# In the second gate/up chunk, the rests of the last ordinary weight pair no longer queue behind the last pair of seven products

## The chip, the core and the metric

The kernel runs on one core of a Trainium2 chip. The metric is the device time of one execution in microseconds (us), as the median of the executions shown. The engines are named as in the profile: PE is TensorE (PEld its weight loads), DVE is VectorE, ACT is ScalarE, POOL is GpSimd and SP is SyncE, which issues most of the transfers.

## What is computed

Two layers of an encoder trunk, for 256 tokens of width 2048 in float32. The part that matters here is the SwiGLU block, with `w_gate` and `w_up` of 2048 x 5632:

```
def swiglu(h, w_gate, w_up, w_down):
    return (jax.nn.silu(h @ w_gate) * (h @ w_up)) @ w_down

def reference(x, w_in, w_o, ..., w_gate, w_up, w_down):
    for l in range(DEPTH):
        h = rms_norm(x, pre_mix_norm[l])
        m = hybrid_mixer(h, l, w_in[l], w_o[l], ...)
        x = x + rms_norm(m, post_mix_norm[l])
        h = rms_norm(x, pre_ffn_norm[l])
        f = swiglu(h, w_gate[l], w_up[l], w_down[l])
        x = x + rms_norm(f, post_ffn_norm[l])
    return x
```

## The kernel before

**Weights.** All weights are laid out in one stream of 128 x 1024 float32 pieces (512 KB), in the order in which they are used. A piece holds 256 rows (`kp`, eight of them) of 512 columns (`c`, the chunk; eleven for gate and up). The stream's index is part of a tile's name. In layer 0, 144 to 159 are the gate and up pieces of chunk 1 in turn, and 160 to 175 those of chunk 2. Layer 1 has the same pattern 392 places further on.

**Rounding.** Each float32 product is made of three products of a rounded part and a rest. For an ordinary piece, `feed` lets ScalarE round it (`hi<-raw`, L310) and VectorE take the difference, the *rest* (`lo<-raw,hi`, L320). `raw` has four buffers, `hi` and `lo` six each. The next piece can be fetched into a `raw` buffer once the rest of the piece in it is made.

**Ordinary pairs and sevens.** An ordinary gate/up pair takes eight blocks of products on TensorE (`eight`, L1255). For some `kp` (in chunk 1: 5 and 6, in chunk 2: 2, 4, 5 and 6) seven products stand for the eight (`seven_products`, L1137 to L1139), as in Strassen's scheme. For these, the up piece `T` arrives in two transfers: a plain one that SP issues (L258), and an accumulation of half the gate piece on top, issued on POOL's queue (L259), which waits for the first. The gate piece is `G` (L231). `mixed_weights` then makes the sums of the two, each with a rounded part and a rest:

- `hi<-T` (ACT L280) and `lo<-T` (DVE L282)
- `T<-T` (DVE L291) and `G<-G,T` (DVE L292), the sums
- `Th<-T` (ACT) and `Tl<-T` (DVE), half a piece, then `Th<-G` and `Tl<-G`, a whole one. The last of the seven products read these.

**Who decides the order.** A scheduler places the instructions of every engine, by its own estimates. `tc.issue_after` keeps an instruction behind another one in this order, without a wait on a semaphore. `held` is a pair of such an instruction and a count: `behind` puts the next ordinary rests, as many as the count, behind it. In chunk 1 the pairs are used in turn, 0 to 7. Pairs 5 and 6 are sevens, pair 7 (pieces 158 and 159) is the last and ordinary one. When the weights of pair 6 have been prepared, `mixed_weights` sets `held` to that piece's last rest, `Tl<-G`, for two rests, which are lo158 and lo159. The set `last_of_row` names the pieces after which this is done: the up piece of pair 6 of chunk 1, one in each layer.

**Other work near by.** For two gate pieces of each chunk, the second and third, POOL makes the rest (`helped`, L313). After the chunk's last seven, `shared_part` (L1178 to L1182) combines the sums that the products share. At the chunk's end VectorE adds these to the accumulators (L1433, L1437), ScalarE applies silu (L1434), and VectorE multiplies (L1439). The result of the chunk before is transposed on TensorE (L1372) near the chunk's end, and ScalarE copies it out of the accumulator bank (L1373).

**Transfers.** `fetch` gives out the transfers in the stream's order, and the scheduler places them on SP. `not_ahead` keeps a transfer of the sevens (`G` and `T`) behind an ordinary one at least six pieces earlier. `put_away` (L396) sends a quarter of the residual to memory once in each of four chunks.

Of the kernel before, what the change touches and what calls it, by code (L numbers as in the profile page):

```python
# [45 lines left out]
NEXT_SEVEN = (5, 6)  # L46
# [34 lines left out]
def weight_order():  # L81

    order = []

    def queue_pair(name, l, kp, c):
        order.append((name, l, kp, c))
        return len(order) - 1

    plan = []
    sevens, plain, own = set(), set(), set()  # L90
    for l in range(L):
        lay = {"in": {}, "o": {}, "gate": {}, "up": {}, "down": {}}
        for n, (ca, cb) in enumerate(PAIRS):
            for kp in IN_ORDER if n else range(KT // 2):
                lay["in"][ca, kp] = queue_pair("w_in", l, kp, ca)
                lay["in"][cb, kp] = queue_pair("w_in", l, kp, cb)
                if kp in IN_NOW[n]:
                    plain.add(lay["in"][cb, kp])
        order_o = [(c, kp) for kp in KP_O for c in (0, 1)]
        order_o += [(c, kp) for kp in LATE_O for c in (2, 3)] + [(c, kp) for c in (2, 3) for kp in LAST_O]  # L100
        lay["order_o"] = order_o
        for c, kp in order_o:
            lay["o"][c, kp] = queue_pair("w_o", l, kp, c)
            if c == 3 and kp in O_SEVEN:
                own.add(lay["o"][c, kp])
        for c in range(FF // CW):
            for kp in gate_order(c):
                lay["gate"][c, kp] = queue_pair("w_gate", l, kp, c)
                lay["up"][c, kp] = queue_pair("w_up", l, kp, c)
                if kp in gate_sevens(c):  # L110
                    sevens.add(lay["up"][c, kp])
        for half in range(2):
            for kp in range(FF // P // 2):
                for c in (2 * half, 2 * half + 1):
                    lay["down"][c, kp] = queue_pair("w_down", l, kp, c)
                if kp in DOWN_SEVEN[half]:
                    sevens.add(lay["down"][2 * half + 1, kp])
        plan.append(lay)
    return order, plan, sevens, plain, own
# [48 lines left out]
def kernel(  # L168
# [35 lines left out]
    order, plan, sevens, plain, own = weight_order()  # L204
# [5 lines left out]
            for n in (1, 2):  # L210
                helped[lay["gate"][c, gate_order(c)[n]]] = n == 1
    newest_seven = [None]
    last_of_row = {lay["up"][1, NEXT_SEVEN[-1]] for lay in plan}

    ready = {}
    raws, loads = [], []
# [47 lines left out]
    def mixed_weights(i):  # L264

        g, u = raws[i - 1], raws[i]
        hi = wpool.tile([P, 2, CW], F32R, tag="hi", bufs=6, name=f"hi{i}")
        lo = wpool.tile([P, 2, CW], F32R, tag="lo", bufs=6, name=f"lo{i}")
        if i in own:
            th = wpool.tile([P, 2, CW], F32R, tag="hi", bufs=6, name=f"Th{i}")  # L270
            tl = wpool.tile([P, 2, CW], F32R, tag="lo", bufs=6, name=f"Tl{i}")
            th2 = mix_pool[0].tile([P, 2 * (S + P)], F32R, tag="ah", bufs=1, name=f"T2h{i}")[:, 0:CW]
            tl2 = mix_pool[0].tile([P, 2 * (S + P)], F32R, tag="al", bufs=1, name=f"T2l{i}")[:, 0:CW]
        else:
            th = mix_pool[0].tile([P, 3, CW], F32R, tag="Th", bufs=1 if i in plain else 2, name=f"Th{i}")
            tl = mix_pool[0].tile([P, 3, CW], F32R, tag="Tl", bufs=1 if i in plain else 2, name=f"Tl{i}")
            th2, tl2 = th[:, 2, :], tl[:, 2, :]

        def split(h, l, w):
            nc.scalar.activation(h, w, AF.Copy)  # L280
            with in_row(i):
                newest_rest[i] = nc.vector.tensor_tensor(out=l, in0=w, in1=h.bitcast(F32), op=ALU.subtract)  # L282

        if i in plain or i in own:
            with after_rests():
                nc.vector.tensor_tensor(out=u[:, 0, :], in0=g[:, 0, :], in1=u[:, 0, :], op=ALU.add)
        split(hi, lo, u)
        t1, b22 = ((hi[:, k, :], lo[:, k, :]) for k in range(2))
        t3, t4 = ((th[:, k, :], tl[:, k, :]) for k in range(2))
        t2 = u[:, 1, :]  # L290
        nc.vector.tensor_tensor(out=t2, in0=t2, in1=u[:, 0, :], op=ALU.subtract)  # L291
        nc.vector.tensor_tensor(out=g, in0=g, in1=t2.unsqueeze(1).to_broadcast([P, 2, CW]), op=ALU.add)  # L292
        split(th2, tl2, t2)
        split(th[:, 0:2, :], tl[:, 0:2, :], g)
        if i in last_of_row:
            held[:] = newest_rest[i], 2
        t2 = th2, tl2
        return {"b22": b22, "t1": t1, "t2": t2, "t3": t3, "t4": t4}

    def feed(upto):  # L300
        fetch(upto)
        while fed[0] < min(upto, len(stream)):
            i = fed[0]
            raw = raws[i]
            if i in sevens or i in plain or i in own:
                ready[i] = mixed_weights(i)
                fed[0] += 1
                continue
            hi = wpool.tile([P, 2, CW], F32R, tag="hi", bufs=6, name=f"hi{i}")
            nc.scalar.activation(hi, raw, AF.Copy)  # L310
            lo = wpool.tile([P, 2, CW], F32R, tag="lo", bufs=6, name=f"lo{i}")
            if i in helped:
                rest = nc.gpsimd.tensor_tensor(out=lo, in0=raw, in1=hi.bitcast(F32), op=ALU.subtract)  # L313
                if helped[i]:
                    tc.add_manual_dep(rest.ins, newest_seven[0].ins.name, AFTER, reason="the shared port")
                ready[i] = (hi, lo)
                fed[0] += 1
                continue
            with behind():
                rest = nc.vector.tensor_tensor(out=lo, in0=raw, in1=hi.bitcast(F32), op=ALU.subtract)  # L320
            ready[i] = (hi, lo)
            fed[0] += 1
            rests.append(rest)
# [21 lines left out]
    held = [None, 0]  # L345
    follows, newest_rest = {}, {}

    def in_row(i):

        return tc.issue_after(follows[i].ins) if i in follows else nullcontext()  # L350
# [8 lines left out]
    def after_rests():  # L359

        return tc.issue_after(rests[-1].ins)
# [826 lines left out]
    for l in range(L):  # L1188
# [27 lines left out]
        for kp in LATE_O[:-1]:  # L1216
            i, j = (plan[l]["o"][c, kp] for c in (2, 3))
# [387 lines left out]
```

## Time and profile before

| What | Value |
|---|---|
| median of 3 runs | 2183.49 us (2182.69 to 2186.39) |
| the profiled execution's own time | 2185.51 us |
| its span, first to last instruction | 2183.8 us |
| granted TensorE clock | 0.999 |
| TensorE busy | 2168.2 us, 99% |
| VectorE busy | 1912.0 us, 88% |
| ScalarE busy | 1392.1 us, 64% |
| GpSimd busy | 256.1 us, 12% |
| read from memory | 460.14 MB, 215 GB/s over the span |

All the details come from the one profiled execution. A row of a timeline has the start in us from the span's beginning, the duration, the engine, the source line, the operation, `out<-in`, the shapes and how many equal instructions are merged (`x4`). In brackets stands how long the engine was idle before it, and what ended that. In the timeline, buffer numbers are left out of the names, so the instructions are told apart by their place.

### The profile page before, as it was taken

Reading aid. Unit: us, or ns where it says so; the run is one execution under the profiler, and the core shown is the slowest. Engines: PE = TensorE matmul, PEld = TensorE weight load, DVE = VectorE, ACT = ScalarE, POOL = GpSimd, SP = SyncE. Lnnn points to the kernel's source line nnn. Section 1 sums busy time; section 2 is a strip of 40 time slices with the busy share of each in tenths; the row PEclk is TensorE's granted clock in tenths of the full one; section 3 lists DMA queues with packets and bytes.
Section 4 is the critical chain, followed back from the end, with each engine's and each line's share of the span. In section 5 each row is a group of like instructions: output and inputs, shape, how many; then the busy total and the mean of one; then the engine's idle time right before and its main releaser. Section 6 shows DMA issues by size and latency. Waiting matters only on the chain.

```text
span 2183.8 us, 28775 instructions
## 1 busy us (share of the span) xinstructions
PE 2168.2 (99%) x9956; PEld 1783.6 (82%) x9956; DVE 1912.0 (88%) x2641; ACT 1392.1 (64%) x2081; POOL 256.1 (12%) x239
## 2 busy tenths in 40 slices
PE   9999999999999999999999999999999999999998
PEld 7888888887888888888878888888888888888886
DVE  7888658889999999999878886588899999999997
ACT  7666665756666666666665666657566666576664
POOL 2100000021222220000010000000222222200000
PEclk9999999999999999999999999999999999999999
DMA  9545555488887777767465555545888877767683
GB/s 336 182 163 174 193 185 177 155 281 247 242 257 229 231 231 236 234 227 254 147 241 174 175 176 186 193 158 179 285 244 237 260 221 230 237 228 242 207 266 100
DMA packets 140274, 470.43 MB, mean 215 GB/s; under 512 B 15952, under 2 KB 16976, under 8 KB 139616
## 3 DMA queue, kind: packets, MB, share of 16 engines
q1 hardware_dynamic: 121952, 436.03, 57.8%
q0 software_dynamic: 17600, 32.02, 8.9%
q8 instruction: 78, 1.28, 0.2%
q10 hardware_dynamic: 576, 0.54, 0.1%
q14 instruction: 68, 0.56, 0.1%
HBM read 460.14 MB, written 8.39 MB: 215 GB/s over the span
## 4 chain that ended last, share of the span: by engine, by line
PE 80%; DVE 11%; issue 3%; DMA 3%; ACT 2%; DVEq 0%; ACTq 0%
PE c L1255 15%; PE in L1137 6%; PE in L1139 6%; PE in L1138 6%; PE dn L1486 4%; PE dn L1487 4%; PE dn L1489 4%; DVE lo L320 3%; PE o L609 2%; PE o L611 2%; PE o L610 2%; DVE Tl L282 2%; PE p L1138 2%; PE c L1138 2%; PE c L1137 2%
## 5 line engine op out<-in xcount | busy, mean ns | idle before, releaser
L320 DVE TENSOR_TENSOR lo<-raw,hi 128x1024 fp32r<-128x1024 f32 x464 | 557.7, 1224 | 105.8 <-ACT hi L310 104.8
L310 ACT ACTIVATE hi<-raw 128x1024 fp32r<-128x1024 f32 x486 | 496.2, 1053 | 86.4 <-DMA raw<-in_weights_in_turn_dram 38.3
L1255 PE MATMUL c<-hi,xF 128*128 128x512 f32 x1344 | 364.0, 392 | 0.9 <-DVE xF L519 0.5
L1255 PEld LDWEIGHTS c<-hi,xF 128*128 128x128 f32 x1344 | 250.2, 188 | 52.6 <-DVE xF L519 1.3
L259 POOL DMA_DIRECT2D T<-in_weights_in_turn_dram x122 | 107.6, 882 | 1394.8 <-PE c L1255 545.2
L1255 PE MATMUL c<-lo,xF 128*128 128x512 f32 x672 | 207.3, 390 | 0.0
L280 ACT ACTIVATE Th<-G 128x1024 fp32r<-128x1024 f32 x122 | 128.8, 1056 | 76.6 <-DVE G L292 75.3
L1486 PE MATMUL dn<-hi,jh 128*128 128x512 f32 x416 | 162.0, 389 | 0.0
L1487 PE MATMUL dn<-lo,jh 128*128 128x512 f32 x416 | 161.8, 389 | 0.0
L280 ACT ACTIVATE Th<-T 128x512 fp32r<-128x512 f32 x122 | 77.2, 633 | 130.2 <-DVE T L291 127.3
L282 DVE TENSOR_TENSOR Tl<-G,Th 128x1024 fp32r<-128x1024 f32 x122 | 149.2, 1223 | 11.3 <-ACT Th L280 11.3
L282 DVE TENSOR_TENSOR lo<-T,hi 128x1024 fp32r<-128x1024 f32 x122 | 155.3, 1273 | 0.7 <-ACT hi L280 0.6
L310 ACT ACTIVATE hi<-G 128x1024 fp32r<-128x1024 f32 x122 | 128.4, 1052 | 36.1 <-DMA G<-in_weights_in_turn_dram 34.5
L292 DVE TENSOR_TENSOR G<-G,T 128x1024 f32<-128x1024 f32 x122 | 148.9, 1221 | 1.8
L1255 PEld LDWEIGHTS c<-lo,xF 128*128 128x128 f32 x672 | 126.0, 188 | 26.3
L320 DVE TENSOR_TENSOR lo<-G,hi 128x1024 fp32r<-128x1024 f32 x104 | 127.0, 1221 | 11.8 <-ACT hi L310 11.7
L280 ACT ACTIVATE hi<-T 128x1024 fp32r<-128x1024 f32 x122 | 128.0, 1049 | 13.3 <-PE c L1139 10.3
L1137 PE MATMUL in<-hi,xT 128*128 128x512 f32 x328 | 131.0, 401 | 0.7 <-ACT hi L942 0.7
L1137 PE MATMUL in<-hi,xI 128*128 128x512 f32 x328 | 131.2, 401 | 0.0
L1138 PE MATMUL in<-lo,xI 128*128 128x512 f32 x328 | 128.0, 390 | 0.3 <-DVE lo L320 0.3
L1489 PE MATMUL dn<-hi,jl 128*128 128x512 f32 x416 | 128.1, 389 | 0.0
L1139 PE MATMUL in<-hi,xI 128*128 128x512 f32 x328 | 128.0, 391 | 0.0
(487 smaller groups left out, 4925.9 us busy)
## 6 DMA issues: line engine op xcount, KB each, us to landing
raw<-in_weights_in_turn_dram SPq DMA_DIRECT2D x498, 512.0 KB, 4.7
T<-in_weights_in_turn_dram SPq DMA_DIRECT2D x122, 512.0 KB, 5.5
G<-in_weights_in_turn_dram SPq DMA_DIRECT2D x122, 512.0 KB, 5.6
T<-in_weights_in_turn_dram POOLq DMA_DIRECT2D x122, 256.0 KB, 5.9
GU<-in_weights_in_turn_dram SPq DMA_DIRECT2D x32, 512.0 KB, 6.5
V<-in_weights_in_turn_dram SPq DMA_DIRECT2D x8, 512.0 KB, 3.8
away_ffn<-x SPq DMA_DIRECT2D x8, 512.0 KB, 8.4
xd<-away_ffn SPq DMA_DIRECT2D x8, 512.0 KB, 8.7
```

What stands on the lines that cost most here:

```text
L280: nc.scalar.activation(h, w, AF.Copy)
L282: newest_rest[i] = nc.vector.tensor_tensor(out=l, in0=w, in1=h.bitcast(F32), op=ALU.subtract)
L292: nc.vector.tensor_tensor(out=g, in0=g, in1=t2.unsqueeze(1).to_broadcast([P, 2, CW]), op=ALU.add)
L310: nc.scalar.activation(hi, raw, AF.Copy)
L320: rest = nc.vector.tensor_tensor(out=lo, in0=raw, in1=hi.bitcast(F32), op=ALU.subtract)
L1137: nc.tensor.matmul(a, sh, hi, start=first, stop=False, skip_group_check=open_sums[0])
L1138: nc.tensor.matmul(a, sh, lo, start=False, stop=False, skip_group_check=open_sums[0])
L1139: return nc.tensor.matmul(a, sl, hi, start=False, stop=last, skip_group_check=open_sums[0])
L1255: nc.tensor.matmul(a, stat[part], w[j][:, kk, :], start=first and kk + n == 0, stop=last and kk == 1 and n == 2)
L1486: nc.tensor.matmul(accs[c, t], sh, hi[:, kk, :], start=first, stop=False, skip_group_check=open_sums[0])
L1487: nc.tensor.matmul(accs[c, t], sh, lo[:, kk, :], start=False, stop=False, skip_group_check=open_sums[0])
L1489: nc.tensor.matmul(accs[c, t], sl, hi[:, kk, :], start=False, stop=last, skip_group_check=open_sums[0])
```

## The change

The two lines that set `held` in `mixed_weights` go, and the set that they ask with them. The rests of pair 7 in chunk 1 then carry no order of their own relative to `Tl<-G` of pair 6, and the scheduler places them by its estimates. The other uses of `held` stay.

```diff
@@ -210,7 +210,6 @@
     newest_seven = [None]
-    last_of_row = {lay["up"][1, NEXT_SEVEN[-1]] for lay in plan}
 
@@ -292,8 +291,6 @@
         split(th2, tl2, t2)
         split(th[:, 0:2, :], tl[:, 0:2, :], g)
-        if i in last_of_row:
-            held[:] = newest_rest[i], 2
         t2 = th2, tl2
```

No instruction is added or removed. The lines behind the edit move up by one to three, so L282 becomes L281, L320 becomes L317, and L242 becomes L241.

On VectorE, in layer 0, near the end of chunk 1's preparation, before the change. `T_4334` and `G_4421` are the pieces of pair 6; `lo_4471` and `lo_4477` are lo158 and lo159, and the last two lo160 and lo161 of chunk 2:

```order
579 L282 TENSOR_TENSOR lo_4428<-T_4334,hi_4427 128x1024
580 L291 TENSOR_TENSOR T_4334<-T_4334 128x512
581 L292 TENSOR_TENSOR G_4421<-G_4421,T_4334 128x1024
582 L282 TENSOR_TENSOR Tl_4430<-T_4334,Th_4429 128x512
583 L282 TENSOR_TENSOR Tl_4430<-G_4421,Th_4429 128x1024
584 L320 TENSOR_TENSOR lo_4471<-raw_4467,hi_4469 128x1024
585 L320 TENSOR_TENSOR lo_4477<-raw_4473,hi_4475 128x1024
586 L320 TENSOR_TENSOR lo_4504<-raw_4500,hi_4502 128x1024
587 L320 TENSOR_TENSOR lo_4513<-raw_4509,hi_4511 128x1024
```

The same place on VectorE after the change:

```order
579 L281 TENSOR_TENSOR lo_4428<-T_4334,hi_4427 128x1024
580 L290 TENSOR_TENSOR T_4334<-T_4334 128x512
581 L291 TENSOR_TENSOR G_4421<-G_4421,T_4334 128x1024
582 L281 TENSOR_TENSOR Tl_4430<-T_4334,Th_4429 128x512
583 L317 TENSOR_TENSOR lo_4471<-raw_4467,hi_4469 128x1024
584 L281 TENSOR_TENSOR Tl_4430<-G_4421,Th_4429 128x1024
585 L317 TENSOR_TENSOR lo_4477<-raw_4473,hi_4475 128x1024
586 L317 TENSOR_TENSOR lo_4504<-raw_4500,hi_4502 128x1024
587 L317 TENSOR_TENSOR lo_4513<-raw_4509,hi_4511 128x1024
```

One rest, lo158, has changed places with `Tl<-G`; lo159 stays where it was. Layer 1 has the same exchange, and nothing else moves on VectorE.

On SyncE's queue, behind the last transfer issued for chunk 1, before the change (all but the one to `away_ffn0` fetch weights, and the first number in a name is the stream's index):

```order
187 L231 DMA G164_4606<-in_weights_in_turn_dram 128x1024
188 L242 DMA raw162_4545<-in_weights_in_turn_dram 128x1024
189 L242 DMA raw163_4551<-in_weights_in_turn_dram 128x1024
190 L258 DMA T169_4612<-in_weights_in_turn_dram 128x1024
191 L396 DMA away_ffn0_4651<-x0_0_0_2459 128x1024
192 L242 DMA raw166_4653<-in_weights_in_turn_dram 128x1024
193 L258 DMA T171_4659<-in_weights_in_turn_dram 128x1024
194 L242 DMA raw167_4662<-in_weights_in_turn_dram 128x1024
195 L231 DMA G168_4696<-in_weights_in_turn_dram 128x1024
196 L258 DMA T173_4702<-in_weights_in_turn_dram 128x1024
197 L231 DMA G170_4738<-in_weights_in_turn_dram 128x1024
```

The same place on SyncE after the change:

```order
187 L230 DMA G164_4606<-in_weights_in_turn_dram 128x1024
188 L241 DMA raw162_4545<-in_weights_in_turn_dram 128x1024
189 L230 DMA G168_4696<-in_weights_in_turn_dram 128x1024
190 L241 DMA raw163_4551<-in_weights_in_turn_dram 128x1024
191 L257 DMA T169_4612<-in_weights_in_turn_dram 128x1024
192 L393 DMA away_ffn0_4651<-x0_0_0_2459 128x1024
193 L241 DMA raw166_4653<-in_weights_in_turn_dram 128x1024
194 L257 DMA T171_4659<-in_weights_in_turn_dram 128x1024
195 L241 DMA raw167_4662<-in_weights_in_turn_dram 128x1024
196 L257 DMA T173_4702<-in_weights_in_turn_dram 128x1024
197 L230 DMA G170_4738<-in_weights_in_turn_dram 128x1024
```

G168 has moved ahead by six places, to right behind raw162, and raw163, T169, the residual's quarter, raw166, T171 and raw167 stand one place later. A little further on, G172 and raw176 change places (G172 now second). Layer 1 has both moves too. TensorE, ScalarE and GpSimd keep their orders.

## The prediction

> **What bounds the kernel now.** I read the page first, then what TensorE waits for, then one engine after the other around the second gate/up chunk of layer 0.
>
> ```profile
> span 2183.8 us, 28775 instructions
> PE 2168.2 (99%) x9956; PEld 1783.6 (82%) x9956; DVE 1912.0 (88%) x2641; ACT 1392.1 (64%) x2081; POOL 256.1 (12%) x239
> ```
>
> TensorE is busy for 99% of the span. No edit to another engine's order can bring more than the idle time in front of TensorE's instructions. That idle time, from the start of the first gate/up stage (395 us) to the end, by what ended it (total, times, longest, in us; two of seven rows):
>
> ```profile
> PE p L1138 <- DVE Tl L282: 2.7, 4, 1.3
> PE c L1255 <- ACT act L1373: 0.5, 1, 0.5
> ```
>
> The same places in TensorE's timeline (start, duration, idle before in brackets), with three rows from ahead of them:
>
> ```profile
> 466.58 0.62 PE L1255 MATMUL c<-lo,xF 128*128 128x512 f32 x2
> ...
> 475.42 0.39 PE L1138 MATMUL p<-Tl,sh 128*128 128x512 f32 x1
> ...
> 476.32 0.39 PE L1139 MATMUL c<-Th,xF 128*128 128x512 f32 x1
> ...
> 483.73 0.96 PE L1255 MATMUL c<-hi,xF 128*128 128x512 f32 x3 [0.45 <-ACT act L1373]
> 519.71 0.50 PE L1138 MATMUL p<-Tl,sh 128*128 128x512 f32 x1 [1.28 <-DVE Tl L282]
> 1604.66 0.50 PE L1138 MATMUL p<-Tl,sh 128*128 128x512 f32 x1 [0.38 <-DVE Tl L282]
> 1683.22 0.50 PE L1138 MATMUL p<-Tl,sh 128*128 128x512 f32 x1 [0.76 <-DVE Tl L282]
> 1725.21 0.50 PE L1138 MATMUL p<-Tl,sh 128*128 128x512 f32 x1 [0.32 <-DVE Tl L282]
> ```
>
> Five waits lie behind the edited place: 0.45 + 1.28 in layer 0 and 0.38 + 0.76 + 0.32 in layer 1, together 3.19 us. That is the most the change can win. The last three come from VectorE's rests being late, the first from a ScalarE copy.
>
> VectorE's timeline around the edit (chunk 1 ends near 483, chunk 2 near 525):
>
> ```profile
> 469.87 0.69 DVE L282 TENSOR_TENSOR Tl<-T,Th 128x512 fp32r<-128x512 f32 x1
> 471.29 1.23 DVE L282 TENSOR_TENSOR Tl<-G,Th 128x1024 fp32r<-128x1024 f32 x1 [0.73 <-ACT Th L280]
> 472.43 4.62 DVE L320 TENSOR_TENSOR lo<-raw,hi 128x1024 fp32r<-128x1024 f32 x4
> ...
> 483.23 1.23 DVE L320 TENSOR_TENSOR lo<-raw,hi 128x1024 fp32r<-128x1024 f32 x1 [3.46 <-ACT hi L310]
> 484.38 0.68 DVE L1433 TENSOR_TENSOR w<-c,w 128x512 f32<-128x512 f32 x1
> ...
> 488.36 3.63 DVE L282 TENSOR_TENSOR lo<-T,hi 128x1024 fp32r<-128x1024 f32 x1 [0.19 <-ACT hi L280]
> 492.03 0.69 DVE L291 TENSOR_TENSOR T<-T 128x512 f32<-128x512 f32 x1
> 492.81 1.23 DVE L292 TENSOR_TENSOR G<-G,T 128x1024 f32<-128x1024 f32 x1
> ...
> 518.43 1.22 DVE L282 TENSOR_TENSOR Tl<-G,Th 128x1024 fp32r<-128x1024 f32 x1
> ```
>
> The four rests in the 4.62 us row are lo158 to lo161: (4.62 - 1.22) / 3 = 1.13 us from one start to the next. The order rows in the section on the change show that the first of them moves ahead of `Tl<-G`. From 483.23 on VectorE has almost no idle time until the TensorE wait at 519.71, so that wait begins with lo163 at 483.23.
>
> ScalarE, SyncE's queue and the chain that ended last, over the same stretch:
>
> ```profile
> 469.26 1.05 ACT L310 ACTIVATE hi<-raw 128x1024 fp32r<-128x1024 f32 x1
> 470.21 1.04 ACT L280 ACTIVATE Th<-G 128x1024 fp32r<-128x1024 f32 x1
> ...
> 477.42 1.06 ACT L310 ACTIVATE hi<-raw 128x1024 fp32r<-128x1024 f32 x1 [2.85 <-DMA raw<-in_weights_in_turn_dram]
> 482.14 1.06 ACT L310 ACTIVATE hi<-raw 128x1024 fp32r<-128x1024 f32 x1 [3.66 <-DMA raw<-in_weights_in_turn_dram]
> 483.11 1.05 ACT L1373 COPY act<-actT_ps 128x512 f32<-128x512 f32 x2
> ```
>
> ```profile
> 473.73 1.77 SPq L242 DMA_DIRECT2D raw<-in_weights_in_turn_dram  x2
> 482.05 0.33 SPq L231 DMA_DIRECT2D G<-in_weights_in_turn_dram  x1
> ```
>
> ```profile
> 472.43 0.79 DVE lo L320
> 474.81 7.22 DMA raw<-in_weights_in_turn_dram
> 482.14 1.06 ACT hi L310
> 483.20 0.48 ACT act L1373
> ```
>
> This is the chain that matters. SyncE issues raw162 at 473.73, when lo158 ends and frees its buffer, and raw163 at 474.81, after lo159. Raw163 lands 7.22 us later, at 482.03. ScalarE takes its instructions in order, so hi163 at 482.14 holds the copy at 483.11, for which TensorE waits 0.45 us. VectorE also stands behind lo163.
>
> **The change, part by part.** *What leaves.* hi158 is ready at 469.26 + 1.05 = 470.31. `Tl<-T` ends at 470.56, and the next instruction can start about 0.09 earlier (1.22 - 1.13), at 470.47. So lo158 fits into the 0.73 us in which VectorE waits for Th: it starts at 470.47 instead of 472.43, which is 1.96 us earlier.
>
> *What is delayed.* `Tl<-G` starts at 470.47 + 1.13 = 471.60 instead of 471.29 and ends at 472.83. Its next reader is the matmul at 475.42, so 2.6 us of other products cover the 0.31 us: cost 0. Without that cover it would cost 0.31 per layer. No wait is added elsewhere. lo158's buffer was last read by the products at 466.58 at the latest, which end an ordinary pair.
>
> *What follows at once.* lo159 starts at 471.60 + 1.13 = 472.73 instead of 472.43 + 1.13 = 473.56, 0.83 earlier; lo160 and lo161 the same. POOL's lo162, which must wait for hi162 and for the last of the seven products, does not come before 476.32 + 0.39 = 476.71, and lo161 is done at 472.73 + 2 x 1.13 + 1.22 = 476.21, so these two do not meet.
>
> *SyncE's queue.* Raw162 goes out 1.96 earlier, raw163 only 0.83 earlier. G168 now stands between them and needs no wait, and T169, raw166 and T171 come one place later behind it. The rate of the transfers, in 40 slices of 0.5 us from 470 to 490:
>
> ```profile
> GB/s 0 0 0 0 0 0 0 0 33 49 246 352 377 148 0 147 344 336 254 188 320 401 410 426 418 410 418 410 442 410 401 418 410 442 401 406 328 307 299 287
> ```
>
> Four us of silence come first, since the queue's head waits for lo158. Then follow some 6 us of a slow start, and then a steady 410 to 420 GB/s. One 512 KB transfer at 418 GB/s is 524,288 / 418,000 = 1.25 us. Raw162 landed at about 477.3 (hi162 at 477.42) and raw163 4.7 us later, 3.5 us more than one such transfer: the slow start delays whatever stands second. I take this delay as going with the start of the burst, because layer 1, below, shows it as well. Then raw163, now third, lands 1.96 earlier and 1.25 later: -0.71 us. This is bounded by -4.2 (the 3.5 does not appear again, -0.71 - 3.5) and +1.25 (the early start is worth nothing). I take -0.71 as both ends of the sum are measured.
>
> The Trainium skill's "DMA: Bandwidth & Descriptors" fits a transfer with 2.0 us plus bytes / 436 GB/s, 3.2 us here; raw162's 477.3 - 473.73 = 3.6 is near that, raw163's 7.22 is not, so by that fit the chain above would not exist, and the measurement decides.
>
> *T171 and POOL.* VectorE's L292 overwrites G164, which POOL's lo164 reads, and lo164 stands in POOL's queue behind the issue of T171's second half, which waits for T171's first landing. POOL in layer 0 and layer 1:
>
> ```profile
> L259 POOLq EVENT_SEMAPHORE  x1: 17/17/17, 487.0 to 487.0; - x1
> ...
> 488.20 2.71 POOL L313 TENSOR_TENSOR lo<-G,hi 128x1024 fp32r<-128x1024 f32 x1
> ```
>
> ```profile
> L259 POOLq EVENT_SEMAPHORE  x1: 17/17/17, 1573.0 to 1573.0; - x1
> ...
> 1574.23 2.89 POOL L313 TENSOR_TENSOR lo<-G,hi 128x1024 fp32r<-128x1024 f32 x1
> ```
>
> T171 also moves by -1.96 + 1.25 = -0.71 (landing near 486.3). lo164 then starts at 487.5, VectorE's lo165 (3.63 us beside POOL, 1.22 alone) at 487.65, and L292 at 492.81 - 0.71 = 492.10. The rest of that stretch of VectorE has no idle time to lose, so `Tl<-G` ends at 519.65 - 0.71 = 518.94.
>
> *Layer 0.* TensorE loses the 0.45 wait (hi163 at 481.4, copy at 482.4). Without waits it would reach the last `Tl` at 519.71 - 1.28 - 0.45 = 517.98, and it goes on when VectorE lets it, at 519.00: 0.71 earlier than now.
>
> *Layer 1.* The same places there:
>
> ```profile
> 1567.41 1.06 ACT L310 ACTIVATE hi<-raw 128x1024 fp32r<-128x1024 f32 x1 [4.02 <-DMA raw<-in_weights_in_turn_dram]
> ...
> 1574.89 2.77 DVE L291 TENSOR_TENSOR T<-T 128x512 f32<-128x512 f32 x1
> 1577.76 1.23 DVE L292 TENSOR_TENSOR G<-G,T 128x1024 f32<-128x1024 f32 x1
> ```
>
> hi163's twin waits 4.02 us for its weights, as in layer 0, and lo164's twin ends at 1577.1, just before L292. VectorE moves by -0.71 again. The wait of 0.38 goes, the next one becomes 0.76 - 0.33, and TensorE again gains 0.71. The 0.32 at 1725.21 stays.
>
> *Sum.* 2 x -0.71 = -1.42 us, 2182.4 for the span and 2184.1 against the profiled execution's own 2185.51. That execution lies 2.02 above the median of 2183.49, so against the median: **2182.1**. This is 0.07%; a measurement here can tell from no change about 0.2%, or 4.4 us (the three times before spread over 2182.69 to 2186.39).
>
> **The rivals.** *A, the slow start does not come back.* G168 fills the 1.9 us between raw162 and raw163, and the transfers run at the steady rate by the time raw163 is reached. Raw163 is then early enough for ScalarE and VectorE, and L292 waits only for lo164. VectorE gains the 1.73 and 1.46 that are asked for, all five waits go, and 2183.49 - 3.19 = 2180.3. For it: lo165 would be done before POOL's lo164 starts, which alone is worth 492.81 - 490.91 = 1.9. Against it: both layers show the late raw163. The fit of the Trainium skill's page on DMA, named above, would give this case.
>
> *B, given back.* The gain is used up before 519, or by a weight that lands later in the following chunks; no wait is longer than before: 2183.5. For it: VectorE is busy 88% of the span, and the waits at 1683 and 1725 show that it is late again after an early start. Against it: everything there follows from VectorE's own releases, and those move with it.
>
> *C, slower.* The early start is worth nothing, because the slow phase is tied to the place and not to the burst's start, or grows with what is queued in it; G168 then costs its place. Raw163 and T171 land 1.25 later, TensorE's wait at 483.73 becomes 1.70, L292 and the `Tl` at 519.71 and 1604.66 come 1.25 later, in each layer: 2183.49 + 2.5 = 2186.0. It decides from the point where T171 lands after 487.0 and 1573.0. If it lands 2.2 late in both layers, the loss passes 0.2%, at 2187.9. For it: the delay behind raw162 is three transfers long, for reasons that no row shows.
>
> That the change does not do what it says is excluded: the order rows show lo158 moved.
>
> **How the numbers follow.** Forecast 0.50, A 0.12, B 0.13, C 0.25, of which 0.13 passes 2187.9. The low end is A with a little scatter, 2180.0; the high end is the point where C passes 0.2%, 2188.0. Faster by over 0.2% needs more than all five waits, so only scatter on top of A: 0.05. Slower by over 0.2%: the far half of C, 0.13. Same: 0.82.
>
> **What would show it.** Right: VectorE's wait for Th of 0.73 before `Tl<-G` gone, raw162 issued near 471.8 with a G right behind it, raw163 landing near 481.3, lo164 on POOL near 487.5, the 0.45 gone and the 1.28 down to about 1.0. Wrong: T171's landing after 487.0, the copy L1373 later than 483.11, or a new wait of TensorE between 525 and 1096.

## The result, and the profile after

The changed kernel takes **2181.65 us** at the median of 22 runs (2179.25 to 2183.16). The kernel before takes 2183.97 beside it (22 runs, 2182.05 to 2186.91). The ratio is 0.9986, with a 95% interval of 0.9980 to 0.9992: 3.1 us less, between 1.7 and 4.4. In a second series it took 2180.91 against 2184.03, ratio 0.9985 (0.9976 to 0.9994). By the medians alone it is 2.3 us less. So the sign of the forecast, -1.42, was right, and the gain is larger, about twice by the ratio and 1.6 times by the medians.

The page of the changed kernel:

```profile
span 2180.7 us, 28777 instructions
PE 2167.5 (99%) x9956; PEld 1785.6 (82%) x9956; DVE 1911.3 (88%) x2641; ACT 1394.6 (64%) x2081; POOL 252.5 (12%) x239
```

What TensorE waits for from 395 us on (total, times, longest; two of six rows):

```profile
PE p L1135 <- DVE Tl L281: 1.2, 2, 0.8
PE c L1252 <- DVE xF L516: 0.5, 2, 0.2
```

The row of the copy L1373 is gone, and of the four waits for a `Tl` two are left. TensorE's timeline around them:

```profile
517.95 0.39 PE L1136 MATMUL p<-Th,sl 128*128 128x512 f32 x1
518.18 0.39 PE L1134 MATMUL p<-Th,sh 128*128 128x512 f32 x1
519.00 0.50 PE L1135 MATMUL p<-Tl,sh 128*128 128x512 f32 x1 [0.43 <-DVE Tl L281]
519.33 0.40 PE L1136 MATMUL p<-Th,sl 128*128 128x512 f32 x1
519.57 0.40 PE L1134 MATMUL c<-Th,xF 128*128 128x512 f32 x1
...
1681.07 0.50 PE L1135 MATMUL p<-Tl,sh 128*128 128x512 f32 x1 [0.75 <-DVE Tl L281]
```

The waits of 0.45, 0.38 and 0.32 are gone, 1.28 has become 0.43, and 0.76 has stayed at 0.75. That is 1.18 us where it was 3.19.

VectorE of the changed kernel in layer 0:

```profile
472.34 0.69 DVE L281 TENSOR_TENSOR Tl<-T,Th 128x512 fp32r<-128x512 f32 x1
472.94 1.22 DVE L317 TENSOR_TENSOR lo<-raw,hi 128x1024 fp32r<-128x1024 f32 x1
474.07 1.22 DVE L281 TENSOR_TENSOR Tl<-G,Th 128x1024 fp32r<-128x1024 f32 x1
475.21 3.49 DVE L317 TENSOR_TENSOR lo<-raw,hi 128x1024 fp32r<-128x1024 f32 x3
...
482.86 1.23 DVE L317 TENSOR_TENSOR lo<-raw,hi 128x1024 fp32r<-128x1024 f32 x1 [1.45 <-ACT hi L307]
...
488.00 1.23 DVE L281 TENSOR_TENSOR lo<-T,hi 128x1024 fp32r<-128x1024 f32 x1 [0.19 <-ACT hi L279]
489.26 2.76 DVE L290 TENSOR_TENSOR T<-T 128x512 f32<-128x512 f32 x1
492.11 1.23 DVE L291 TENSOR_TENSOR G<-G,T 128x1024 f32<-128x1024 f32 x1
...
517.72 1.22 DVE L281 TENSOR_TENSOR Tl<-G,Th 128x1024 fp32r<-128x1024 f32 x1
```

lo158 (472.94) fills the idle 0.73, and `Tl<-G` follows it without a pause. In this execution VectorE reached `Tl<-T` at 472.34, in the one before at 469.87, and in a second profile of the changed kernel at 468.45. So the clock time of a row can't be compared between two traces here. Below, places are counted from the start of this `Tl<-T`.

SyncE's queue, ScalarE, the event of T171's landing for which POOL's queue waits, and POOL's rest, over the same stretch:

```profile
474.19 0.33 SPq L241 DMA_DIRECT2D raw<-in_weights_in_turn_dram  x1
474.56 0.43 SPq L230 DMA_DIRECT2D G<-in_weights_in_turn_dram  x1
476.46 0.33 SPq L241 DMA_DIRECT2D raw<-in_weights_in_turn_dram  x1
```

```profile
477.55 1.06 ACT L307 ACTIVATE hi<-raw 128x1024 fp32r<-128x1024 f32 x1 [0.52 <-DMA raw<-in_weights_in_turn_dram]
481.77 1.06 ACT L307 ACTIVATE hi<-raw 128x1024 fp32r<-128x1024 f32 x1 [3.16 <-DMA raw<-in_weights_in_turn_dram]
482.74 1.06 ACT L1370 COPY act<-actT_ps 128x512 f32<-128x512 f32 x2
```

```profile
L258 POOLq EVENT_SEMAPHORE  x1: 17/17/17, 487.5 to 487.5; - x1
```

```profile
488.65 2.82 POOL L310 TENSOR_TENSOR lo<-G,hi 128x1024 fp32r<-128x1024 f32 x1
```

Raw162 goes out 1.85 us after the start of `Tl<-T` (474.19 - 472.34). Before it was 473.73 - 469.87 = 3.86, so it is 2.01 earlier. G168 stands behind it. T171 lands 487.5 - 472.34 = 15.2 after `Tl<-T`, where it was 17.1, and lo164 again follows the landing by 1.2. (The two event rows have one decimal. The table below goes by the landings themselves, 15.1 and 17.2.)

### The profile page after: what moved, and what is told of

Read it like the earlier page. It is cut to its first block, busy times and chain, and to the rows that moved or that the text cites. A ratio compares the mean times of both kernels' runs of the same rounds, so it can differ in the third digit from the quotient of the medians.

```text
span 2180.7 us, 28777 instructions
## 1 busy us (share of the span) xinstructions
PE 2167.5 (99%) x9956; PEld 1785.6 (82%) x9956; DVE 1911.3 (88%) x2641; ACT 1394.6 (64%) x2081; POOL 252.5 (12%) x239
## 3 DMA queue, kind: packets, MB, share of 16 engines
q8 instruction: 78, 1.28, 0.2%
## 4 chain that ended last, share of the span: by engine, by line
PE 89%; DVE 7%; issue 2%; ACT 1%; DMA 1%; DVEq 0%; ACTq 0%; SPq 0%
PE c L1252 18%; PE in L1134 6%; PE in L1136 6%; PE in L1135 6%; PE dn L1483 4%; PE dn L1486 4%; PE dn L1484 4%; PE p L1135 2%; PE c L1135 2%; PE c L1136 2%; PE c L1134 2%; PE p L1136 2%; PE o L608 2%; PE o L606 2%; PE o L607 2%; PE p L1134 2%
## 5 line engine op out<-in xcount | busy, mean ns | idle before, releaser
L317 DVE TENSOR_TENSOR lo<-raw,hi 128x1024 fp32r<-128x1024 f32 x464 | 557.4, 1222 | 105.0 <-ACT hi L307 102.6
L281 DVE TENSOR_TENSOR Tl<-G,Th 128x1024 fp32r<-128x1024 f32 x122 | 149.1, 1222 | 9.8 <-ACT Th L279 9.8
L281 DVE TENSOR_TENSOR lo<-T,hi 128x1024 fp32r<-128x1024 f32 x122 | 152.3, 1248 | 0.5 <-ACT hi L279 0.4
L279 ACT ACTIVATE hi<-T 128x1024 fp32r<-128x1024 f32 x122 | 128.0, 1049 | 13.1 <-PE c L1136 10.2
L317 DVE TENSOR_TENSOR lo<-G,hi 128x1024 fp32r<-128x1024 f32 x104 | 126.7, 1219 | 10.2 <-ACT hi L307 10.2
L1134 PE MATMUL in<-hi,xT 128*128 128x512 f32 x328 | 131.9, 404 | 0.6 <-ACT hi L939 0.6
L1134 PE MATMUL in<-hi,xI 128*128 128x512 f32 x328 | 131.1, 401 | 0.0
L1136 PE MATMUL in<-hi,xT 128*128 128x512 f32 x328 | 128.4, 393 | 0.0
L1135 PE MATMUL in<-lo,xT 128*128 128x512 f32 x328 | 128.2, 392 | 0.0
```

The costliest lines, as they stand in the source:

```text
L1134: nc.tensor.matmul(a, sh, hi, start=first, stop=False, skip_group_check=open_sums[0])
L1135: nc.tensor.matmul(a, sh, lo, start=False, stop=False, skip_group_check=open_sums[0])
L1136: return nc.tensor.matmul(a, sl, hi, start=False, stop=last, skip_group_check=open_sums[0])
```

## The experiments

Three theories were set up first. T1 is the prediction's: the start of the burst of transfers, and the place in it. T2: VectorE gains its own 0.73 us, and the transfers don't matter. T3: G168 as a filler behind raw162 is what helps. All runs were timed against the kernel before on the same chip, in five rounds. In the tables, "gain" is by the ratio of the runs, times 2184 us, with its interval.

### The first four: start and filler

**g168_early_only**, the kernel before with G168's load put behind raw162:

```diff
+    put_first = {lay["gate"][2, 4] for lay in plan}
...
-                with not_ahead(i):
+                with not_ahead(i), tc.high_priority(offset=5000) if i in put_first else nullcontext():
```

> The kernel before, with G168 alone put right behind raw162 on SyncE's queue, in both layers; VectorE's order is that of before. Three theories are compared, against the kernel before. T1, place and start of the burst: TensorE follows the landing of raw163 and T171, which move with the burst's start and by 1.25 us for each transfer put ahead of them. Here the start stays and G168 is ahead, so both land 1.25 later: the wait behind the ScalarE copy grows from 0.45 to about 1.7, and the time by 2 x 1.25 = 2.5 us. T2, VectorE's own 0.73 us: the change wins because VectorE's idle time is filled, wherever the transfers stand. VectorE is not changed here: 0 us. T3, the filler: what wins is that G168 stands in the slow start of the burst in raw163's stead. Raw163 then lands within 4 us of raw162, as in the changed kernel: 1 to 2 us faster.

Measured: 2182.16 against 2183.59, ratio 0.9999 (0.9990 to 1.0007). G168 put ahead brings nothing that shows, and raw163 landed 4.6 and 4.8 us behind raw162 (layer 0, layer 1), where T3 expected less than 4. The run is not G168 alone, though: on POOL the scheduler also put lo164 ahead of the issue of T171's second half, an exchange that is tried by itself below.

**g168_kept_back**, the changed kernel with G168's load four places later on SyncE, where it is in the kernel before:

```diff
+    kept_back = {lay["gate"][2, 4] for lay in plan}
...
-                with not_ahead(i):
+                with not_ahead(i, 1 if i in kept_back else LEAD):
```

> The changed kernel, with G168 kept at its former place on SyncE's queue, behind raw167, in both layers; VectorE's order is that of the changed kernel. T1: the burst starts 1.96 earlier and nothing is put ahead of raw163 and T171, so T171 lands 1.96 earlier than before and raw163 0.8 to 2.0 earlier; all five waits go, up to 3.2 us faster than before, 0.9 more than the changed kernel. T2: VectorE is that of the changed kernel, so the same time as it, 2.3 faster than before. T3: raw163 stands in the slow start again, 4.7 us behind raw162, and lands only as much earlier as its own issue (0.8): 0.5 to 1.5 faster than before, slower than the changed kernel.

Measured: 2181.05, ratio 0.9988 (0.9979 to 0.9997). Without the filler it gains 2.6 us (0.7 to 4.6), which can't be told from the changed kernel's 3.1; the 0.9 more that T1 expected does not show either. What T3 rests on did not come: raw163 landed 3.9 and 2.6 us behind raw162 and 3.4 and 4.5 earlier than in the kernel before, not 4.7 behind and 0.8 earlier. So T3 falls. (On POOL, T169's second half had moved ahead of lo162 as well.)

**vector_only**, as the last, and raw162 also waits for lo159, so that the transfers start no earlier than before:

```diff
+    waits_on = {lay["gate"][2, 1]: lay["up"][1, 7] for lay in plan}
...
+            if i in waits_on:
+                tc.add_manual_dep(loads[-1].ins, ordinary[waits_on[i]].ins.name, AFTER, ...)
```

> VectorE's order of the changed kernel, SyncE's order of the kernel before, and raw162's transfer also waits for lo159, so that the burst does not start earlier (0.2 us later than before by the sum). T1: no gain, within 0.5 us of before, raw163 and T171 land as before. T2: all of the gain, 2.3 us faster than before. T3: no gain, as T1.

Measured: 2181.98, ratio 0.9995 (0.9987 to 1.0004). VectorE's order alone, as T2 has it, is not shown to gain: 1.1 us, in an interval from -0.9 to 2.8 that still holds T2's 2.3. Nor is it quite alone here, since T171 landed 0.9 and 2.0 earlier than in the kernel before, though raw162 was issued 0.26 later. Beside it, g168_kept_back, whose transfers start 2.27 earlier, took 2181.05 against 2181.98. That speaks for T1, with the exchange on POOL named there as a second difference.

**burst_later**, the kernel before with the same two lines, and raw162 waiting for lo161:

> The kernel before, but raw162's transfer also waits for lo161, three rests further on, so that the burst starts 3.4 us later in both layers; VectorE's order is that of before. T1: raw163 and T171 land 3.4 later, TensorE's waits at the ScalarE copy and at the last rest of chunk 2 grow by that much, 2 x 3.4 = 6.8 us slower (about 2190.8 where before has 2184). T2: 0. T3: as T1.

Measured: 2181.92, ratio 0.9993 (0.9984 to 1.0002). T1 expected a loss here, and it failed in this plain form. The trace shows why the run can't be read by the transfers alone: the scheduler answered the edit on other engines too. On POOL it put lo164 ahead of the issue of T171's second half. On VectorE, whose order was meant to stay, it put an addition of the chunk's end ahead of lo163. T171 landed later than in the kernel before (18.8 and 19.1 after `Tl<-T`, where it was 17.2 and 18.0), and L292 still came earlier (20.6 and 20.8, where it was 22.9 and 22.7). The same exchange had happened in g168_early_only. So POOL's queue had to be tried by itself.

### POOL's queue by itself

U1: what counts is that lo164 stands behind T171's second half in POOL's queue, since L292 waits for lo164. U2: what counts is the landing of raw163 behind a transfer that goes out alone.

**before_again** is the kernel before, unaltered:

> The kernel before, unchanged, for a second profile. If its five waits are the kernel's own, as the prediction took them: about 3 us of waits between 395 and 1800 us again, with 0.3 to 0.6 behind the ScalarE copy in layer 0 and raw163 landing 4.5 to 5.1 us after raw162. If they were an accident of one execution: waits of well under 2 us in sum, and another spacing of the landings.

Measured: 2184.68 against 2184.15, ratio 0.9998 (0.9989 to 1.0007). In its profile, TensorE waits for more than either expectation says:

```profile
PE p L1138 <- DVE Tl L282: 4.1, 6, 1.3
PE c L1255 <- ACT act L1373: 1.3, 1, 1.3
```

That is 5.4 us of such waits, where the first profile had 3.19, and raw163 landed 3.5 and 4.6 us behind raw162. The sum of the waits belongs to an execution, not to the kernel.

**pool_rest_first**, the kernel before with that exchange and nothing else; **pool_rest_first_after**, the changed kernel with it:

```diff
+    rest_first = {lay["up"][2, 5]: lay["gate"][2, 2] for lay in plan}
...
-        nc.gpsimd.dma_start(sums[i][:, 0, :], stream[i - 1][:, 0, :], accum_op=ALU.add)
+        with tc.issue_after(by_pool[rest_first[i]].ins) if i in rest_first else nullcontext():
+            nc.gpsimd.dma_start(sums[i][:, 0, :], stream[i - 1][:, 0, :], accum_op=ALU.add)
...
+                by_pool[i] = rest
```

> The kernel before, with one exchange on POOL in each layer: lo164, POOL's rest of a gate piece, stands ahead of the issue of T171's second half instead of behind it. VectorE, ScalarE and SyncE keep the order of before. U1, POOL's place: VectorE's sum L292 waits for lo164, and lo164 waits in POOL's queue for T171's landing, so lo164 starts as soon as hi164 is made (486.8 instead of 488.2 in layer 0, 1572.1 instead of 1574.2 in layer 1), VectorE is 1.3 and 2 us earlier, the 1.28 and 0.38 waits go, 2 to 2.7 us faster. U2, the burst: only the landing of raw163 counts, by the ScalarE copy and lo163; the time stays within 0.5 us of before.

> The changed kernel with the same exchange on POOL (lo164 ahead of the issue of T171's second half). U1: the changed kernel still has a wait of 0.4 at 519 in layer 0 and its gain is the same VectorE time, so the two gains do not add: 0.4 to 1.2 us faster than the changed kernel, about 3 faster than before. U2: the same time as the changed kernel.

Measured: 2181.88, ratio 0.9988 (0.9979 to 0.9996), and 2179.53, ratio 0.9975 (0.9966 to 0.9984). POOL and then VectorE of pool_rest_first:

```profile
482.30 0.89 POOL L262 DMA_DIRECT2D T<-in_weights_in_turn_dram  x1 [1.65 <-PE c L1259]
485.19 2.40 POOL L316 TENSOR_TENSOR lo<-G,hi 128x1024 fp32r<-128x1024 f32 x1 [2.00 <-ACT hi L313]
487.54 0.87 POOL L262 DMA_DIRECT2D T<-in_weights_in_turn_dram  x1
```

```profile
486.64 2.03 DVE L285 TENSOR_TENSOR lo<-T,hi 128x1024 fp32r<-128x1024 f32 x1 [0.19 <-ACT hi L283]
488.70 0.69 DVE L294 TENSOR_TENSOR T<-T 128x512 f32<-128x512 f32 x1
489.49 1.23 DVE L295 TENSOR_TENSOR G<-G,T 128x1024 f32<-128x1024 f32 x1
```

lo164 now waits for its own rounded part only, and L292 (here L295) comes 489.49 - 469.24 = 20.2 after `Tl<-T`. TensorE has one wait of 0.6 for a `Tl` left:

```profile
PE p L1142 <- DVE Tl L285: 0.6, 1, 0.6
```

This one exchange is worth 2.6 us, by the intervals as much as the whole change, and the two together gain 5.5. So U1's place in POOL's queue counts. Two things of U1 did not come. The first is that the two gains would not add (it expected about 3 us against the kernel before).

The second is that L292 *waits* for lo164. In all 14 traces, in both layers, L292 follows `T<-T` after less than 0.1 us of idle time. What lo164 holds up is the row of VectorE that runs beside it: `lo<-T`, which takes 1.23 us alone, 2.03 here and 3.63 in the kernel before, or `T<-T`, which takes 0.69 alone and 2.76 in the changed kernel. That row ends 1.09 or 0.55 us after lo164 does, and L292 therefore starts 1.9 or 0.64 us after lo164's end, in each of the 28 places. Here lo164 ends at 485.19 + 2.40 = 487.59, and 489.49 is 1.90 later. In the changed kernel it ends at 488.65 + 2.82 = 491.47, and 492.11 is 0.64 later.

**pair_together**, the kernel before with raw162 waiting for lo159, every other engine as before:

> The kernel before, but raw162's transfer also waits for lo159, so that raw162 and raw163 are issued together, 1.1 us later than raw162 is now; POOL, VectorE and ScalarE keep the order of before (on SyncE raw175 and T179, much later, change places). T1, start and place of the burst: everything lands 1.1 later, 2.3 us slower. U2, the lone transfer: what delays raw163 by 3.5 us is that raw162 goes out alone and the next follows 1.1 us later; issued within 0.45 us of it, as in the runs vector_only and burst_later, raw163 lands 1.4 to 2.1 after raw162, so 1.5 to 2 us earlier than before although the burst starts later: the wait of 0.45 goes, VectorE starts chunk 2 up to 1.9 earlier, and the time falls by 1 to 2 us.

Measured: 2184.20, ratio 0.9999 (0.9991 to 1.0007). T1's loss of 2.3 us did not come. U2's landings did, but its gain of 1 to 2 us does not show; the interval, -1.5 to 2.0, does not exclude it. SyncE's queue and ScalarE's two hi rows:

```profile
474.77 0.81 SPq L242 DMA_DIRECT2D raw<-in_weights_in_turn_dram  x2
```

```profile
478.17 1.06 ACT L314 ACTIVATE hi<-raw 128x1024 fp32r<-128x1024 f32 x1 [3.65 <-DMA raw<-in_weights_in_turn_dram]
480.07 1.06 ACT L314 ACTIVATE hi<-raw 128x1024 fp32r<-128x1024 f32 x1 [0.84 <-DMA raw<-in_weights_in_turn_dram]
```

The burst began 1.1 later than in the kernel before, and raw163 landed 2.0 *earlier* (10.1 after `Tl<-T`, not 12.2): the delay of the second transfer is not a constant that goes with the start of the burst.

### G168's place by itself

Last, the term "+1.25 for G168" alone, with all engines' orders held, POOL's too. P is the prediction, Q says that the second one is late with or without a transfer in between.

**keep_g_alone** is the changed kernel with the edit of g168_kept_back and T169's second half tied behind lo162, as it stands in the changed kernel; **keep_g_pool_first** is the same beside pool_rest_first_after. **after_again** and **pool_first_after_again** repeat two kernels unaltered.

> The changed kernel a second time, nothing altered, as the reference for the runs beside it and for a second profile. 2181.7 us at the median, within 1 us. If the waits of TensorE in its profile differ from those of the first profile of the changed kernel by as much as between the two profiles of the kernel before (1.28 against 0.45 at the first place, one more of 0.51), single waits cannot be read as effects, and only the sum of many can.

> The changed kernel with one thing altered: the load of G168 (and its twin in layer 1) keeps the place in SyncE's queue that it has in the kernel before, four loads later; every other engine's order is that of the changed kernel. So the term of the prediction 'G168 ahead costs one transfer' stands alone. Theory P (the prediction): raw163 and T171 land 1.25 us earlier than in the changed kernel, counted from raw162's landing (raw163 at 3.0 and 1.8 in place of 4.22 and 3.04), and the time falls by 2.5 us against the changed kernel run beside it. Theory Q (what stands second is late by the slow start whether or not something stands between): raw163 lands 3.9 to 4.6 after raw162 in layer 0, T171 about 10 after it, and the time is that of the changed kernel within 0.7 us.

> As keep_g_alone, but with POOL's rest lo164 ahead of the issue of T171's second half, as in pool_rest_first_after; against that kernel only G168's place on SyncE's queue differs. T171's landing then no longer decides when lo164 starts. Theory P: raw163 1.25 earlier, but all of TensorE's waits of the stage were gone already, so no more than 0.5 us against pool_rest_first_after (2179.5). Theory Q: the same as pool_rest_first_after within 0.7. Against the kernel before both say 3.5 to 5 us less. This run is a candidate for the best version more than a test.

> pool_rest_first_after a second time, nothing altered, beside the others on one chip: 2179.5 within 1 us, 2.1 less than the changed kernel.

Measured, against 2184.03: 2180.91, 2179.73, 2179.13 and 2178.15. The last has a ratio of 0.9973 (0.9962 to 0.9984). SyncE's queue and ScalarE of keep_g_alone:

```profile
471.25 2.60 SPq L241 DMA_DIRECT2D raw<-in_weights_in_turn_dram  x2
473.89 0.43 SPq L261 DMA_DIRECT2D T<-in_weights_in_turn_dram  x1
```

```profile
474.65 1.06 ACT L312 ACTIVATE hi<-raw 128x1024 fp32r<-128x1024 f32 x1 [0.54 <-DMA raw<-in_weights_in_turn_dram]
477.77 1.06 ACT L312 ACTIVATE hi<-raw 128x1024 fp32r<-128x1024 f32 x1 [2.06 <-DMA raw<-in_weights_in_turn_dram]
```

Without G168 between them raw163 lands 3.1 and 2.7 us behind raw162, and T171 1.0 us earlier than in the changed kernel (table below). P expected 1.25 for both, and Q about none, with raw163 3.9 to 4.6 behind raw162 in layer 0. So Q fails here, and P holds for raw163 in layer 0 but not in layer 1, where it moves by 0.3. In keep_g_pool_first, though, raw163 in layer 0 is 4.2 behind raw162, as Q has it. In time keep_g_alone is ahead of after_again by 1.2 us by the medians and 2.2 by the ratios, and the intervals overlap: a gain is likely, not shown. Where lo164 doesn't wait for T171, keeping G168 back brought nothing (2179.13 against 2178.15). The last run is 1.35 us faster than the 2179.5 expected of it, a little beyond the 1 us allowed.

### All traces on one scale

Places in us after the start of `Tl<-T` of chunk 1's pair 6, layer 0 / layer 1, worked out from the traces:

| kernel | raw162 lands | raw163 lands | T171 lands | lo164 starts | L292 starts | gain, us (95%) |
|---|---|---|---|---|---|---|
| before | 7.4 / 7.2 | 12.2 / 12.3 | 17.2 / 18.0 | 18.3 / 19.2 | 22.9 / 22.7 | - |
| before_again | 8.2 / 7.2 | 11.8 / 11.7 | 17.1 / 17.5 | 18.3 / 18.7 | 22.9 / 22.2 | 0.4 (-1.5 to 2.4) |
| vector_only | 9.6 / 7.2 | 11.0 / 9.3 | 16.3 / 16.0 | 17.5 / 17.2 | 22.1 / 20.7 | 1.1 (-0.9 to 2.8) |
| pair_together | 8.2 / 8.3 | 10.1 / 10.1 | 16.6 / 16.5 | 17.8 / 17.8 | 21.1 / 21.1 | 0.2 (-1.5 to 2.0) |
| g168_early_only | 7.2 / 7.0 | 11.8 / 11.8 | 17.3 / 17.1 | 16.6 / 16.7 | 20.9 / 21.0 | 0.2 (-1.5 to 2.2) |
| burst_later | 10.6 / 10.5 | 12.4 / 12.5 | 18.8 / 19.1 | 16.3 / 16.3 | 20.6 / 20.8 | 1.5 (-0.4 to 3.5) |
| pool_rest_first | 7.8 / 7.2 | 11.1 / 11.8 | 16.4 / 16.9 | 16.0 / 16.7 | 20.2 / 21.0 | 2.6 (0.9 to 4.6) |
| **after** | 5.1 / 5.2 | 9.3 / 8.2 | 15.1 / 14.8 | 16.3 / 16.0 | 19.8 / 19.7 | 3.1 (1.7 to 4.4) |
| after_again | 5.2 / 5.1 | 10.2 / 8.2 | 15.5 / 15.0 | 16.7 / 16.2 | 21.3 / 20.8 | 3.3 (1.3 to 5.2) |
| g168_kept_back | 4.9 / 5.2 | 8.8 / 7.8 | 14.9 / 14.2 | 16.1 / 15.4 | 20.7 / 20.1 | 2.6 (0.7 to 4.6) |
| keep_g_alone | 5.1 / 5.1 | 8.3 / 7.9 | 14.0 / 14.2 | 15.2 / 15.5 | 19.8 / 18.8 | 5.5 (3.5 to 7.6) |
| keep_g_pool_first | 5.1 / 4.9 | 9.4 / 7.8 | 14.8 / 14.3 | 14.8 / 14.9 | 19.1 / 19.2 | 5.0 (2.8 to 7.0) |
| pool_rest_first_after | 5.2 / 5.2 | 9.6 / 8.7 | 15.1 / 15.8 | 14.4 / 13.6 | 18.8 / 17.9 | 5.5 (3.5 to 7.4) |
| pool_first_after_again | 5.1 / 5.2 | 9.6 / 9.3 | 15.3 / 15.3 | 15.4 / 14.2 | 19.8 / 18.5 | 5.9 (3.5 to 8.3) |

On the whole the gain goes with the places of lo164 and L292, whatever was done to move them: over the 13 rows below the first the correlations are 0.89 and 0.88 (0.68 and 0.69 for raw163's and T171's landings), and each us that L292 comes earlier in both layers goes with 1.6 us. It does not hold row by row: with L292 near 21, after_again gains 3.3 and g168_early_only and pair_together 0.2. The places are those of one execution each, the gains those of many. pool_rest_first_after and its repeat, with L292 some 4 us earlier, have the largest gains beside keep_g_alone; the repeat took 2178.15 where the changed kernel beside it took 2180.91.

## Why the prediction was right, and where its size was off

**lo158 into the idle 0.73: right.** 472.94 follows `Tl<-T` by 0.60, as forecast, and raw162 is issued 2.01 earlier (forecast 1.96). The delay of `Tl<-G` cost nothing, and no wait of TensorE stands there.

**The chain through POOL: right, but its last link is another.** lo164 stands behind T171's landing in both kernels (1.2 us in each), and pool_rest_first shows by itself that this place has a price. The prediction ties L292 to lo164 because L292 overwrites what lo164 reads. The traces show VectorE held earlier, in the row that runs beside lo164. Which row that is makes 1.27 us (1.91 - 0.64): in layer 0 it was `lo<-T` before and `T<-T` in the first profile of the change.

**The signs in clock times: not to be read as they stand.** Raw162 was to go out near 471.8 and went out at 474.19, and T171 landed at 487.5, after the 487.0 that was to show the prediction wrong. VectorE as a whole was 2.47 later in this execution (472.34 - 469.87). From the start of `Tl<-T`, raw162 goes out at 1.85, where the forecast had 1.9 (471.8 - 469.87), and T171 lands earlier, not later. lo162 and lo161, which were not to meet, do so in this execution (POOL starts lo162 at 478.70, where lo161 ends, 475.21 + 3.49); no wait of TensorE follows from it.

**"Raw163, now third, lands 1.96 earlier and 1.25 later: -0.71", and the same for T171: this is the step that failed.** By the table, means of two traces and two layers, T171 lands 15.1 after `Tl<-T` instead of 17.4. That is -2.3, not -0.71; lo164 and L292 move by -2.3 too, and raw163 by -3.0.

The pieces of T171's -2.3: raw162 lands 2.36 earlier (forecast 1.96). From raw162's landing to T171's it took 9.9 before, 9.0 in keep_g_alone (9.3 as the mean of the three kernels that keep G168 back) and 9.9 in the changed kernel. So G168's place costs some 0.6 to 1.0 (forecast 1.25; single places scatter over 8.9 to 10.0 with G168 kept back and 9.6 to 10.3 with G168 ahead), and about as much is gained elsewhere, so that T171 moves by as much as raw162. The likely reason, which no run shows by itself, is that raw163 and those behind it are now issued 2.27 us after raw162 instead of 1.08, and less of the slow start falls on them. The silence ahead of the burst is shorter too: by the packets of the weight transfers it lasts 6.9 to 8.0 us in the kernel before, not the four that its view from 470 on shows, and 4.8 to 6.1 in the changed kernel.

The prediction had taken the delay "as going with the start of the burst". In pair_together and vector_only, where the two are issued together (0.45 apart), raw163 comes 1.4 to 2.1 behind raw162. 1.08 apart (before, before_again and pool_rest_first), it is 3.3 to 5.1, and in the three that keep G168 back, 2.27 apart, 2.6 to 4.2. The Trainium skill's "DMA: Bandwidth & Descriptors" (section "Anatomy of one DMA — SWDGE (gpsimd) path") fits a transfer issued on GpSimd's queue with 2.0 us plus bytes / 436 GB/s, which gives an estimate of 3.2 us for 512 KB. On SyncE's queue raw162, first of its burst, took 3.3 in the changed kernel (474.19 to 477.45, hi162 at 477.55) and agrees; raw163 took 5.2 and does not.

**"That is the most the change can win", 3.19: wrong as a limit.** pool_rest_first_after gains 5.5 by its ratio. (Four of the five waits, not the last three alone, are for a `Tl`, as the row of four shows.) One reason is that the list is of one execution; before_again's has 5.4. The other is that a wait costs more than its idle time. Matmuls follow each other here every 0.23 us (517.95 to 518.18). Across the wait at 519.00 it is 0.82 and then 0.33: (0.82 + 0.33) - 2 x 0.23 = 0.69, where the trace shows a wait of 0.43. So 0.26 more is lost: 0.16 because the idle time is counted from the end of the matmul ahead, 0.39 after its start, and not from where the next would start (0.39 - 0.23), and 0.10 at the next matmul (0.33 - 0.23).

Where before and pool_rest_first are laid side by side matmul by matmul, each wait of before that the other lacks moves the two apart by 0.27 to 0.31 more than its idle time: 0.72 for the 0.45, 1.59 for 1.28, 0.66 for 0.38, 0.59 for 0.32. Places with 0.03 to 0.14 idle (517, 617, 699, 1767), which the list in the prediction left out, lose 0.2 to 0.3 more as well.

With -2.3 in place of -0.71 VectorE gives each layer more than the 1.73 and 1.46 asked for, and after_again has none of the five waits (the last two rows of what TensorE waits for):

```profile
PE c L1253 <- DVE xF L517: 0.5, 2, 0.2
PE in L1136 <- DVE lo L318: 0.3, 1, 0.3
```

The first profile kept 0.43 and 0.75, so a single wait can't be read as an effect of the edit. How much is left differs from one execution to the next, as it does for the kernel before: its second profile shows 1.28 at the place where the first had 0.45:

```profile
484.49 0.96 PE L1255 MATMUL c<-hi,xF 128*128 128x512 f32 x3 [1.28 <-ACT act L1373]
...
520.83 0.50 PE L1138 MATMUL p<-Tl,sh 128*128 128x512 f32 x1 [1.28 <-DVE Tl L282]
```

**The rivals.** A (3.19 us less) came nearest in size by the ratio; by the medians, 2.3, it and the forecast are about equally far off. All five waits are gone in one of the two profiles. Its mechanism holds by half: raw163 in layer 1 lands 3.0 and 3.1 behind raw162, but 4.2 and 5.0 in layer 0. lo165 (`lo<-T`) runs unhindered ahead of lo164 in the first profile (488.00, 1.23 us), but not in the second (3.73), and lo164 still waits for T171. B (given back) is out: both intervals lie below no change. C (G168 costs its place) named a cost that exists, but the early start was not worth nothing, and T171 landed earlier, not later. The outcome stays within the 0.2% that the prediction took as the least that can be told from no change; with 22 runs of each, 0.14% could.

**Left open.** g168_early_only brings L292 1.8 earlier and gains 0.2 (-1.5 to 2.2), pair_together likewise 1.6 and 0.2. The line through the 13 rows gives 1.9 and 1.6 there, inside both intervals, but it runs 1.1 below zero at the place of the kernel before, so either something besides L292's place counts or the scatter is of that size. after_again, with an early start of the burst, gains more at the same place; that the early start has a worth of its own is possible and not shown. The scheduler's other exchange, of G172 and raw176 a little later, was not tried by itself. In g168_early_only the copy L1373 also stops TensorE for 0.39 in layer 1, since raw163 lands no earlier there.

## What to carry to other kernels

Follow a late tensor operation back through the in-order queue in which it stands: here a rest on POOL waited for a transfer that it doesn't use, because the issue of that transfer's second half stood ahead of it, and exchanging the two was worth as much as the whole change. The late operation need not be the one that is held: here it was a row of another engine, lengthened beside the rest. When an edit moves a transfer, ask what the gap to the transfer ahead of it becomes, not only how many stand ahead. And price a stall of a busy engine at more than its idle time: many short ones can add up to more than the list of waits shows.

## What the hardware showed that was not expected

- After 4.8 to 10.7 us without weight transfers, the first 512 KB transfer of the burst took 3.1 to 3.9 us in 26 of 28 places. The second took 6.1 to 7.3 when issued 1.08 us behind it (before, before_again, pool_rest_first), 4.7 to 4.9 when 0.45 behind it (pair_together, burst_later and one layer of vector_only, 6.4 in the other) and 3.7 to 5.2 when 2.27 behind it with nothing between. Why the middle distance is the worst no run shows.
- A stall of TensorE costs some 0.2 to 0.3 us beyond its idle time in these float32 products, whether it lasts 0.03 or 1.28 us.
- VectorE's `lo<-T` took 1.23 us alone and between 1.37 and 3.99 beside POOL's lo164, and it ended 1.09 us after lo164 each time, as if nearly all of its work were done only then. `T<-T`, 0.69 alone, took 2.76 to 2.92 and ended 0.55 after lo164.
